# Normalising and transposing the second half of the rows in the head, and storing raw queries from ScalarE's queue

## The chip, the cores and the metric

The kernel runs on one core of a Trainium2 chip. The metric is the device time of one launch in microseconds; a time given for a kernel is the median of its runs. The engines are named as in the profile: PE is TensorE (PEld its weight loads), DVE is VectorE, ACT is ScalarE, POOL is GpSimd, SP is SyncE, which here does nothing but issue DMAs.

## The reference

One layer of a transformer block on 1024 rows of 1024 features, all in float32, batch 1: three residual steps, each behind an RMS norm.

```python
x = x + _hybrid_mixer(_rms_norm(x, norm1_g[l]), w_in[l], ...)
x = x + _memory_xattn(_rms_norm(x, norm2_g[l]), mem, ...)
x = x + _sq_relu_mlp(_rms_norm(x, norm3_g[l]), w_ff_in[l], w_ff_out[l])
```

The hybrid mixer first projects the normed rows with `w_in` (1024 x 1760), and splits the result:

```python
proj = h @ w_in
c_q, c_kv, k_idx, w_idx, q_nsa, kv_nsa, g_nsa = jnp.split(proj, splits, axis=-1)
c_q = _rms_norm(c_q, dsa_cq_g)
c_kv = _rms_norm(c_kv, dsa_ckv_g)
q_d = _rope(_rms_norm((c_q @ w_dsa_uq).reshape(B, L, DSA_HEADS, D), dsa_qn_g), pos)
k_d, v_d = jnp.split(c_kv @ w_dsa_ukv, 2, axis=-1)
q_i = _rope((c_q @ w_idx_q).reshape(B, L, IDX_HEADS, IDX_DIM), pos)
q_n = _rope(_rms_norm(q_nsa.reshape(B, L, NSA_HEADS, D), nsa_qn_g), pos)
```

Then every block of 128 rows attends in four ways: over 256 keys that an indexer selects by top-k (`q_i` scores, `q_d` attends), over keys compressed from blocks of 32, over 16 selected blocks of 64, and over a window of 512. All are causal: a block of rows needs keys of its own and of earlier rows alone. The result goes through `w_out`. Memory cross-attention (4 heads, 256 memory rows) and an MLP with squared ReLU (width 4096) follow.

## The kernel before

**Tiles and parts.** The 1024 rows are 8 tiles of 128 rows, and these are two parts of four: `PARTS = ((0, 4), (4, 4))`. Part 0 is projected first, in a stretch called the head here, with pools of its own (`p1` in SBUF, `ps1` in PSUM). Then these pools close, the main pools open, and two streams are interleaved: attention of tile after tile (`attend`), and a `fill` of everything else: projection of part 1 (in a pool `p2`), the memory stage, what lies between, and a first part of the MLP. Attention of tiles 4 to 7 is held until part 1 is projected. After that comes the tail, mostly MLP.

**Order of the work.** Each stream is a Python generator that yields the price of what it has just issued, and the streams are merged by these prices: `alternate` takes from the stream that is behind, `chain` runs one after the other, `drain` runs one out, and `together` (from L110) lets the fill run up to a pace beside attention, or alone while attention is held. A planner at build time then orders the instructions of each engine by its own estimate of times. On the chip each engine, and each engine's DMA queue, works through its own list in order: a DMA that waits for its data holds every DMA behind it on the same queue.

**project(pool, part, pe, st)**, from L370, does one part:

- The gain of the norm is loaded, broadcast to all partitions (L337, 512 KB). Then for each of four tiles, x is loaded (L375, 512 KB) and `norm_T` runs: ACT squares and sums (L285), DVE scales the sum (L229), POOL raises it to the power -1/2 (L231), DVE multiplies by that and by the gain (L287), PE transposes in eight blocks of 128 x 128 (L274), and ACT and DVE copy the two halves from PSUM (in part 0 split into a high and a low f32r part, L235 and L236; in part 1 kept whole as f32, L278 and L280).
- Eleven constants are loaded (L384 to L394).
- The columns of `w_in` are multiplied in this order: keys and values to be compressed; `c_q`, then `c_kv` with the indexer's key and the gates; keys and values of the selected blocks and of the window, with `compress` beside (part 0) or behind (part 1); `w_dsa_ukv`; NSA queries with `k_prep` (the keys' norms and rotation); then `w_dsa_uq` and `w_idx_q`. Matrix multiplications are at L218. Part 0 uses three multiplications of split operands; part 1 multiplies whole f32 weights (loaded at L265 into buffers named wlo and whi; one step shows as two instructions).
- Raw queries go out through `stage_q` (L398 to L403): ACT copies each tile's 128 x 256 result from PSUM to a buffer `st` (L401), and after the fourth tile SP stores the buffer, 512 KB, to DRAM (L403). Six such stores belong to each part. `st` has two buffers in `p1` and one in `p2`.

Attention reads the stored queries back: `q_prep` (from L560) loads `qin` on SP (L564), normalises and rotates it on ACT, POOL and DVE (L574 to L584), and PE transposes it (L590).

The part of the kernel that calls all this, before the change:

```python
drain(project(p1, 0, pe, st))
...
yield from project(p2, part, pe, st)
```

Of the kernel before, what the change touches and what calls it, by code (L numbers as in the profile page):

```python
# [26 lines left out]
PARTS = ((0, 4), (4, 4))  # L27
# [56 lines left out]
def drain(gen):  # L84
    for _ in gen:
        pass
# [80 lines left out]
def build(nc, tc, I, C, out):  # L167
    v, s, g, te = nc.vector, nc.scalar, nc.gpsimd, nc.tensor
    ctx = ExitStack()
    W = {n: I[n][0] for n in I}  # L170
# [4 lines left out]
    at_pool = tc.tile_pool(name="at", bufs=1, side="right", reuse_waits="tile")  # L175
    at = at_pool.__enter__()
    p1_pool, p1_psum = tc.tile_pool(name="p1", bufs=1, reuse_waits="tile"), tc.tile_pool(name="ps1", bufs=1, space=PSUM)
    p1 = p1_pool.__enter__()
    psum.update(pool=p1_psum.__enter__(), n=PSUMS["p1"])

# [4 lines left out]
    def ring(pool, tag, shape, dt=F32):  # L185
        n = RINGS[pool.name if isinstance(pool.name, str) else "dn"][tag]
        return pool.tile(shape, dt, tag=tag, name=tag, bufs=n)

    def row(ap):
        return ap[None, :]  # L190
# [91 lines left out]
    def norm_T(pool, x_t, gb, xs):  # L282
        ss = small(pool, "nss", 1)
        xn = ring(pool, "x4", [P, DM])
        s.activation(xn, x_t, AF.Square, accum_out=ss)  # L285
        r = rsqrt_of(pool, ss, DM, 1, "n")
        v.scalar_tensor_tensor(xn, x_t, r[:, 0:1], gb, op0=ALU.mult, op1=ALU.mult)  # L287
        to_T(pool, xn, xs, DM // P)
# [11 lines left out]
    def gemm(pool, xs, nk, nt, wsrc, chunks, consume):  # L300

        for ci, parts in enumerate(chunks):
            w = sum(n for _, n in parts)
            gr = []
            for k0 in range(0, nk, KG):
                kn = min(KG, nk - k0)
                srcs, o = [], 0
                for c0, n in parts:
                    srcs.append((lambda r, o=o, n=n: r[:, :, o:o + n],
                                 wsrc[k0 * P:(k0 + kn) * P, c0:c0 + n].rearrange("(k p) n -> p k n", p=P)))  # L310
                    o += n
                ws = load_w(pool, [P, kn, w], *srcs) if len(xs) == 2 else load_whole(pool, [P, kn, w], *srcs)
                gr += [[x[:, k, :] for x in ws] for k in range(kn)]
            for t in range(nt):
                pt = pst(TAGS[pool.name][0], [P, w])
                for k in range(nk):
                    if len(xs) == 1:
                        mm(pt, xs[0](t, k), gr[k][0], k == 0, k == nk - 1)
                        continue
                    wh, wl = gr[k]  # L320
                    xh, xl = xs[0](t, k), xs[1](t, k)
                    mm(pt, xh, wh, k == 0, False)
                    mm(pt, xh, wl, False, False)
                    mm(pt, xl, wh, False, k == nk - 1)
                consume(ci, t, pt)
                yield nk * (5 - len(xs)) * w / 2400.0

    def xT(pool, nt, whole=False):

        parts = [pool.tile([P, DM // P, nt * P], F32 if whole else F32R, tag="x" + n, name="x" + n)  # L330
                 for n in ("h" if whole else "hl")]
        return (parts, [lambda t, k, x=x: x[:, k, t * P:(t + 1) * P] for x in parts],
                lambda t: [x[:, :, t * P:(t + 1) * P] for x in parts])

    def gain(pool, src, tag="x4"):
        gb = ring(pool, tag, [P, DM])
        nc.sync.dma_start(gb, row(src).to_broadcast([P, DM]))  # L337
        return gb

    def gain2(pool, src):  # L340
        gs = [ring(pool, "h", [P, 512]) for _ in range(2)]
        for i, gb in enumerate(gs):
# [16 lines left out]
    qraw = [[[dr.tile([P, n, 256], F32, tag=f"q{k}{t}{c}", name=f"q{k}{t}{c}") for c in range(2)] for t, n in PARTS]  # L359
            for k in range(3)]  # L360
# [4 lines left out]
    xo_dr = [dr.tile([P, 512], F32, tag=f"xo{t}", name=f"xo{t}") for t in range(NT)]  # L365


    def project(pool, part, pe, st):
        t0, nt = PARTS[part]
        gb1 = gain(pool, W["norm1_g"])  # L370
        whole = part > 0
        _, xf, xt_of = xT(pool, nt, whole)
        for t in range(nt):
            x_t = ring(pool, "x4", [P, DM])
            nc.sync.dma_start(x_t, I["x"][0, (t0 + t) * P:(t0 + t + 1) * P, :])  # L375
            norm_T(pool, x_t, gb1, xt_of(t))
            yield 1.0
        cq = [ring(pool, "c8", [P, nt, 2, P], F32 if whole else F32R) for _ in xf]
        ckv = [ring(pool, "c4", [P, nt, P], F32 if whole else F32R) for _ in xf]
        kraw = [ring(pool, "kraw", [P, 6, 64]) for t in range(nt)]  # L380
# [15 lines left out]
        qst = []  # L396

        def stage_q(k, c, t, pt):  # L398
            if t == 0:
                qst[:] = [ring(pool, "st", [P, nt, 256])]  # L400
            s.activation(qst[0][:, t, :], pt, AF.Copy)  # L401
            if t == nt - 1:
                nc.sync.dma_start(qraw[k][part][c], qst[0])  # L403

        def consume(ci, t, pt):
            T = t0 + t
# [20 lines left out]
            if ci in (2, 3):  # L427
                stage_q(1, ci - 2, t, pt)
# [17 lines left out]
        def w_in(chunks, first):  # L446
            return gemm(pool, xf, DM // P, nt, W["w_in"], chunks,
                        lambda ci, t, pt: consume(ci + first, t, pt))
# [33 lines left out]
        yield from w_in([[(968, 256)]], 4)  # L482
        yield from w_in([[(0, 256)], [(256, 200), (1736, 24)]], 0)
        pair_ = (w_in([[(1224, 256)], [(1480, 256)]], 5), compress(pool, part, KT, pe, st, ctab))
        yield from (alternate if part == 0 else chain)(*pair_)
        yield from gemm(pool, [lambda t, k, c=c: c[:, t, :] for c in ckv], 1, nt,
                        W["w_dsa_ukv"], [[(0, 128)]], consume_kv)
        yield from alternate(w_in([[(456, 256)], [(712, 256)]], 2), k_prep())
        for k, name in ((0, "w_dsa_uq"), (2, "w_idx_q")):
            yield from gemm(pool, [lambda t, k, c=c: c[:, t, k, :] for c in cq], 2, nt,  # L490
                            W[name], [[(0, 256)], [(256, 256)]],
                            lambda ci, t, pt, k=k: stage_q(k, ci, t, pt))
# [568 lines left out]
    def pe_stack():  # L1061
        pe = p1.tile([P, 2, 32], F32R, tag="pe", name="pe")
        pe2 = ring(p1, "relu", [P, 2, 2, 64])
        for j in range(2):
            nc.sync.dma_start(pe2[0:32, :, j, :], W["nsa_cmp_pe"].rearrange("k l d -> l k d"))
        pp = pst("M", [P, 2, 32])
        for kv in range(2):
            te.transpose(pp[:, kv, :], pe2[0:32, kv, :, :].rearrange("p a d -> p (a d)"), ident[0:32, 0:32])
        s.activation(pe, pp, AF.Copy)
        v.tensor_tensor(pe[64:128], pp[64:128], pe[64:128], op=ALU.subtract)  # L1070
        return pe

    st = {
        "K": at.tile([P, 6, L], F32R, tag="K", name="K"),
        "V": [at.tile([P, NT, 2, 2, 64], F32R, tag=f"V{b}", name=f"V{b}") for b in range(2)],
        "Vd": at.tile([P, NT, 2, 64], F32R, tag="Vd", name="Vd"),
        "Kc": {},
        "Vc": {},
        "cT": [at.tile([64, 2, 64], F32, tag=f"cT{kv}", name=f"cT{kv}") for kv in range(2)],
        "cb": [at.tile([64, 1], F32, tag=f"cb{kv}", name=f"cb{kv}") for kv in range(2)],  # L1080
        "wi": at.tile([P, NT, 8], F32, tag="wi", name="wi"),
# [5 lines left out]
        v.memset(st["cT"][kv], 0.0)  # L1087
    pe = pe_stack()
    plan["w"] = PLAN_HEAD
    drain(project(p1, 0, pe, st))  # L1090
    plan["w"] = PLAN_MAIN
    p1_psum.__exit__(None, None, None)
    p1_pool.__exit__(None, None, None)
# [4 lines left out]
    projected = []  # L1098

    def fill():  # L1100
        for part in range(1, len(PARTS)):
            with tc.tile_pool(name="p2", bufs=1, reuse_waits="tile") as p2:
                yield from project(p2, part, pe, st)
            projected.append(part)
        dn = dn_pool.__enter__()
        yield from memory(dn)
        yield 1, PACES[1]
        yield from between(dn, 0, 2, {}, False)
        yield 3, PACES[2]
        x2s = {}  # L1110
        yield from between(dn, 2, 2, x2s, True)
        yield 3, PACES[3]
        yield from mlp(dn, 0, 4, x2s)
        yield 5, PACES[4]
        yield from between(dn, 4, 2, {}, False)

    rest = fill()
    together(attend(aw, st), rest, projected)
    aw_pool.__exit__(None, None, None)
# [32 lines left out]
```

## Time and profile before

| | |
|---|---|
| median of 3 runs | 1833.72 us (1833.55 to 1837.51) |
| profiled execution | 1835.75 us, its span 1833.9 us |
| PE busy | 1726.9 us, 94% of the span |
| ACT, DVE, POOL busy | 59%, 51%, 49% |
| mean granted TensorE clock | 0.970 |
| DMA | 187.50 MB, mean 102 GB/s |

PE busy is the time in which at least one matmul is under way. A row of an engine's timeline gives the start, the duration, the engine, the line and operation, out<-in by the names in the program, shapes and a count, and in brackets the idle time before it with what ended it. A row of groups gives the busy time and the mean duration in ns, then the idle time just before. A row of DMA issues gives the count, the KB of each and the median time from issue to landing. SPq is the DMA queue of SP.

### The profile page before, as it was taken

What the parts mean: (1) busy time and instruction counts of PE and PEld (TensorE: products, weight loads), DVE (VectorE), ACT (ScalarE), POOL (GpSimd) and SP (SyncE); (2) the same over time, 40 slices, a digit from 0 to 9 for tenths busy, and PEclk for the clock granted to TensorE, in tenths of its full rate; (3) what the DMA queues carried; (4) which work ended last, traced back from release to release, by engine and by line L of the source; (5) the groups of instructions that cost most, each with busy time, mean ns of one, the idle gap of its engine ahead of it and who ended that gap; (6) DMA issues with size and microseconds to landing.
All of it is one profiled execution on the core that took longest, in us unless ns stands there. A gap on an engine that the chain in (4) does not pass through costs nothing. (4 is left out here: it accounts for less than half of the span.)

```text
span 1833.9 us, 28049 instructions
## 1 busy us (share of the span) xinstructions
PE 1726.9 (94%) x9262; PEld 1474.2 (80%) x9262; DVE 936.1 (51%) x2353; ACT 1074.6 (59%) x2687; POOL 895.0 (49%) x1034
## 2 busy tenths in 40 slices
PE   5996999889989998999999999999999799999999
PEld 5995988777878787778887788888988578787787
DVE  4553766575684678466664656646523422222222
ACT  4444658889588669955797457994412323333332
POOL 2364657446262244677676576662111144454443
PEclk9997998999999999999999999999989799999999
DMA  8224512256335320222112112125394222222232
GB/s 203 70 87 160 103 34 79 78 193 180 122 112 162 120 81 24 73 81 71 64 63 91 54 65 75 60 79 185 99 288 131 71 69 92 92 93 93 94 99 98
DMA packets 180081, 187.50 MB, mean 102 GB/s; under 512 B 34656, under 2 KB 149088, under 8 KB 179936
## 3 DMA queue, kind: packets, MB, share of 16 engines
q1 hardware_dynamic: 172000, 175.23, 30.8%
q0 software_dynamic: 7936, 10.49, 2.2%
q8 instruction: 73, 1.20, 0.3%
q14 instruction: 72, 0.59, 0.1%
HBM read 164.69 MB, written 20.97 MB: 101 GB/s over the span
## 5 line engine op out<-in xcount | busy, mean ns | idle before, releaser
L249 POOL TENSOR_TENSOR wlo<-wraw,whi 128x512 fp32r<-128x512 f32 (+1 forms) x230 | 308.5, 1347 | 278.7 <-ACT whi L244 247.6
L244 ACT ACTIVATE whi<-wraw 128x512 fp32r<-128x512 f32 (+2 forms) x289 | 181.1, 628 | 247.4 <-PE psS L218 147.1
L218 PE MATMUL psD<-whi,xh 128*128 128x256 f32 (+1 forms) x704 | 193.8, 359 | 3.6 <-ACT whi L244 2.9
L218 PE MATMUL psD<-wlo,xh 128*128 128x256 f32 (+1 forms) x704 | 194.8, 357 | 0.8 <-DMA wlo<-in_w_in_dram 0.8
L236 DVE TENSOR_TENSOR pl<-psPT,ph 128x512 fp32r<-128x512 f32 (+1 forms) x232 | 142.2, 621 | 78.2 <-ACT ph L235 75.4
L218 PE MATMUL psD<-whi,h 128*128 128x512 f32 x512 | 174.3, 404 | 1.8 <-POOL h L1037 1.0
L688 ACT ACTIVATE S<-S,mn 128x128 f32<-128x128 f32 (+7 forms) x192 | 142.7, 744 | 41.5 <-DVE mn L686 40.3
L218 PE MATMUL psS<-whi,h 128*128 128x512 f32 x512 | 162.1, 392 | 5.1 <-DVE b L899 5.1
L693 POOL TENSOR_SCALAR S<-S,sums,gi 128x640 f32<-128x640 f32 (+7 forms) x128 | 107.7, 850 | 106.7 <-DVE sums L691 99.0
L235 ACT ACTIVATE ph<-psPT 128x512 fp32r<-128x512 f32 (+1 forms) x232 | 122.8, 540 | 60.9 <-PE psPT L703 54.5
L249 DVE TENSOR_TENSOR wlo<-wraw,whi 128x512 fp32r<-128x512 f32 (+1 forms) x59 | 64.3, 1090 | 166.9 <-ACT whi L244 166.8
L218 PEld LDWEIGHTS psD<-whi,xh 128*128 128x128 f32 x704 | 134.0, 198 | 14.3 <-ACT whi L244 3.3
L218 PEld LDWEIGHTS psD<-wlo,xh 128*128 128x128 f32 x704 | 134.8, 197 | 12.5 <-DMA wlo<-in_w_in_dram 1.2
L703 PE MATMUL psPT<-c_ident,S 128*128 128x128 f32 x816 | 132.3, 279 | 8.3 <-DVE ql L236 4.2
L899 DVE TENSOR_TENSOR b<-psS,b 128x512 f32<-128x512 f32 (+1 forms) x80 | 50.0, 635 | 152.6 <-PE psS L218 152.6
L218 PEld LDWEIGHTS psS<-whi,h 128*128 128x128 f32 x512 | 96.1, 188 | 29.3 <-DVE b L899 9.3
L218 PE MATMUL psS<-K,qh 128*128 128x384 f32 (+3 forms) x288 | 113.5, 397 | 5.6 <-DVE mn L686 2.8
L218 PEld LDWEIGHTS psD<-whi,h 128*128 128x128 f32 x512 | 95.6, 190 | 23.7 <-DVE b L899 1.5
L703 PEld LDWEIGHTS psPT<-c_ident,S 128*128 128x128 f32 x816 | 98.1, 143 | 18.9 <-POOL S L693 5.6
L218 PE MATMUL psD<-wlo,h 128*128 128x512 f32 x256 | 102.5, 404 | 1.3 <-POOL wlo L249 1.3
L218 PE MATMUL psD<-xh,wlo 128*128 128x512 f32 x256 | 101.5, 398 | 0.0
L899 DVE TENSOR_TENSOR b<-psD,b 128x512 f32<-128x512 f32 (+1 forms) x112 | 63.2, 572 | 74.5 <-PE psD L218 73.0
(299 smaller groups left out, 4647.4 us busy)
## 6 DMA issues: line engine op xcount, KB each, us to landing
wraw<-in_w_ff_in_dram SPq DMA_DIRECT2D x128, 256.0 KB, 2.7
wraw<-in_w_ff_out_dram SPq DMA_DIRECT2D x128, 256.0 KB, 2.6
whi<-in_w_out_dram SPq DMA_DIRECT2D x32, 256.0 KB, 5.0
wlo<-in_w_out_dram SPq DMA_DIRECT2D x32, 256.0 KB, 4.6
wraw<-in_w_in_dram SPq DMA_DIRECT2D x24, 256.0 KB, 3.1
q<-st SPq DMA_DIRECT2D x12, 512.0 KB, 2.6
qin<-q SPq DMA_DIRECT2D x44, 128.0 KB, 2.3
x<-in_x_dram SPq DMA_DIRECT2D x8, 512.0 KB, 5.2
```

The lines of the kernel that those rows point to most:

```text
L218: te.matmul(o, a, b, start=start, stop=stop)
L235: s.activation(hi, src, AF.Copy)
L236: v.tensor_tensor(lo, src, hi, op=ALU.subtract)
L244: s.activation(hi, raw, AF.Copy)
L249: (v if l == "v" else g).tensor_tensor(lo, raw, hi, op=ALU.subtract)
L688: s.activation(S, S, AF.Exp, bias=low, scale=-1.0, accum_out=sums[:, hh:hh + 1])
L693: g.tensor_scalar(Ss[hh], Ss[hh], sums[:, hh:hh + 1], 1.0 if gate is None else gate[:, hh:hh + 1], op0=ALU.mult, op1=ALU.mult)
L703: te.transpose(p2[:, j, hh, :], S[:, (c + j) * P:(c + j + 1) * P], ident)
L899: v.tensor_tensor(dst, pt, dst, op=ALU.add)
```

## The change

Three things are done:

1. The norm and the transposes of part 1 are taken out of `project` into a generator `normed`. The head norms tiles 0 to 3 first, and then runs `normed` for tiles 4 to 7 as a third stream beside the projection of the keys and values of the selected blocks and of the window, and beside `compress`. The transposed rows of tiles 4 to 7 (`xf1`, 16 KB per partition) lie in a new pool `pre`, which stays open until part 1 is projected. The fill's `project` gets `xf1` and begins with its constants.
2. The gain of the norm is loaded once rather than twice.
3. The stores of raw queries, all twelve, are issued from ACT's DMA queue rather than SP's.

```diff
+    pre_pool = tc.tile_pool(name="pre", bufs=1, reuse_waits="tile")
+    pre = pre_pool.__enter__()
     p1 = p1_pool.__enter__()
...
-    def project(pool, part, pe, st):
+    def normed(pool, part, gb1, xt_of):
         t0, nt = PARTS[part]
-        gb1 = gain(pool, W["norm1_g"])
-        whole = part > 0
-        _, xf, xt_of = xT(pool, nt, whole)
         for t in range(nt):
             x_t = ring(pool, "x4", [P, DM])
             nc.sync.dma_start(x_t, I["x"][0, (t0 + t) * P:(t0 + t + 1) * P, :])
             norm_T(pool, x_t, gb1, xt_of(t))
             yield 1.0
+
+    def project(pool, part, pe, st, xf, beside_it):
+        t0, nt = PARTS[part]
+        whole = part > 0
...
             if t == nt - 1:
-                nc.sync.dma_start(qraw[k][part][c], qst[0])
+                s.dma_start(qraw[k][part][c], qst[0])
...
-        yield from (alternate if part == 0 else chain)(*pair_)
+        yield from (alternate if part == 0 else chain)(*pair_, *beside_it)
...
-    drain(project(p1, 0, pe, st))
+    gb1 = gain(p1, W["norm1_g"])
+    _, xf0, xt_of0 = xT(p1, PARTS[0][1])
+    _, xf1, xt_of1 = xT(pre, PARTS[1][1], True)
+    drain(normed(p1, 0, gb1, xt_of0))
+    drain(project(p1, 0, pe, st, xf0, [normed(p1, 1, gb1, xt_of1)]))
...
     def fill():
-        for part in range(1, len(PARTS)):
-            with tc.tile_pool(name="p2", bufs=1, reuse_waits="tile") as p2:
-                yield from project(p2, part, pe, st)
-            projected.append(part)
+        with tc.tile_pool(name="p2", bufs=1, reuse_waits="tile") as p2:
+            yield from project(p2, 1, pe, st, xf1, [])
+        projected.append(1)
+        pre_pool.__exit__(None, None, None)
```

## The prediction

> **What bounds the kernel now.** I read the busy table first, then windows of 20 us, then the instructions around the one deep dip.
>
> ```profile
> span 1833.9 us, 28049 instructions
> PE 1726.9 (94%) x9262; PEld 1474.2 (80%) x9262; DVE 936.1 (51%) x2353; ACT 1074.6 (59%) x2687; POOL 895.0 (49%) x1034
> 140.00:160.00 20.00, 7.24 (x50) 6.27 (x49) 3.27 (x8) 4.79 (x12) 5.19 (x6) 0.73 0.58 192
> 160.00:180.00 20.00, 18.30 (x84) 15.56 (x85) 10.21 (x40) 11.27 (x35) 13.72 (x25) 0.76 0.51 174
> 340.00:360.00 20.00, 17.35 (x87) 13.22 (x85) 7.86 (x17) 19.40 (x65) 7.73 (x12) 1.00 0.16 63
> 360.00:380.00 20.00, 16.90 (x76) 12.67 (x76) 14.41 (x51) 14.64 (x44) 3.80 (x6) 0.91 0.38 136
> 380.00:400.00 20.00, 16.16 (x84) 13.70 (x83) 14.33 (x42) 17.62 (x53) 11.07 (x17) 0.83 0.77 256
> ```
>
> TensorE bounds it: 94% busy, 107 us idle in all. A window row gives its length, then PE, PEld, DVE, ACT and POOL busy, the granted clock, the DMA share and GB/s. The dip at 140:160 is the seam, where the head (projection of tiles 0 to 3) has ended and the fill (projection of tiles 4 to 7) has to begin. The three rows from 340 are the stretch where attention waits for that second projection: ACT, at 19.40 of 20, is the busiest engine there, and PE loses 2.65 + 3.10 + 3.84 us. The seam in detail (start, duration, engine, line, out<-in, count, then idle before and its releaser):
>
> ```profile
> 144.76 0.28 PE L218 MATMUL psD<-whi,c 128*128 128x256 f32 x1
> 156.43 1.09 PE L274 MATMUL psM<-c_ident,x 128*128 128x128 f32 x4 [11.39 <-DVE x L287]
> 158.20 1.12 PE L274 MATMUL psM<-c_ident,x 128*128 128x128 f32 x4 [0.69 <-ACT xh L278]
> 160.10 2.07 PE L218 MATMUL psD<-wlo,xh 128*128 128x256 f32 x4 [0.78 <-DMA wlo<-in_w_in_dram]
> 163.68 1.06 PE L590 MATMUL psPT<-c_ident,qd 128*128 128x128 f32 x4
> 144.88 1.21 ACT L401 ACTIVATE st<-psD 128x256 f32<-128x256 f32 x4 [2.30 <-DMA q<-st]
> 132.30 14.14 SPq L403 DMA_DIRECT2D q<-st  x5
> 146.54 0.37 SPq L337 DMA_DIRECT2D x<-in_norm_g_dram  x1
> 146.97 0.78 SPq L375 DMA_DIRECT2D x<-in_x_dram  x1
> 149.25 0.43 SPq L386 DMA_DIRECT2D pc<-in_c_ccos_dram  x1
> 150.19 3.54 SPq L394 DMA_DIRECT2D pc<-in_nsa_kn_g_dram  x4
> 155.20 0.43 SPq L265 DMA_DIRECT2D wlo<-in_w_in_dram  x1
> ```
>
> The head's last matmul ends at 145.04. SP stands from 132.30 in five raw-query stores, each held by its last ACT copy; only behind them go the gain, x, eleven constants and the first weight (155.20). x then needs landing, square, power, multiply, transpose. PE idles 11.39 + 0.69 + 0.78 = 12.9 us.
>
> **The change, part by part.** The sums are made against the profiled execution: span 1833.9 us, 1835.75 with what lies around it, 2.0 above the median of 1833.72. I apply the difference to the median.
>
> Moved norms. Their prices in the head, where tiles 0 to 3 do the same:
>
> ```profile
> L285 ACT ACTIVATE x<-x 128x1024 f32<-128x1024 f32 x4 | 4.2, 1058 | 6.6 <-DMA x<-in_x_dram 6.6
> L287 DVE SCALAR_TENSOR_TENSOR x<-x,nr,x 128x1024 f32<-128x1024 f32 x4 | 6.2, 1545 | 1.8 <-POOL nr L231 1.8
> 40.00:60.00 20.00, 20.00 (x179) 20.00 (x178) 12.52 (x33) 10.88 (x35) 8.59 (x10) 1.00 0.71 142
> 60.00:80.00 20.00, 20.00 (x178) 20.00 (x178) 10.21 (x33) 9.28 (x31) 7.18 (x8) 1.00 0.09 28
> ```
>
> Per tile some 1.6 us of DVE and 1.8 of ACT with one copy each, in windows where these have 7 to 11 us of 20 free; the four x loads (SP, 0.8 us at most each) find a DMA share of 0.09 at 60:80. Those cost nothing, covered by PE's own matmuls; without that cover a tile's chain would show as at the seam. The 32 transposes take PE itself, which is full: eight took 1.09 + 1.12 us at half clock, hence about 1.07 at full, 4.3 us in all. The head ends 4.3 us later, near 149.3, and the fill does 4.3 us less: 0 in sum. A head bubble is bounded by 0 and 1.7 us (6.6 over four, what each load kept ACT waiting in that row); I take 0, as the later loads find quieter queues. The second gain load (0.37 us of SP, 512 KB) goes; it was hidden among the seam's other issues.
>
> The seam itself. What is late next: constants and weights are still issued after the head, since only norms and x loads were moved. The stores leave SP's queue, so SP no longer waits for ACT in order. But in the program as built, one of the last constants still waits for the landing of the head's last raw-query store (the DMAs share a fixed set of completion semaphores, and this one's previous user is that store); already before, four L394 issues took 3.54 us where single ones take 0.43. Counting from the head's last matmul: last copy 1.05 (146.09 minus 145.04), store issue 0.35, landing 2.6, four constants 1.7, weight issue 0.4 and landing 3.2: 9.3 us. The stores' and weights' rows, and the chain that follows:
>
> ```profile
> q<-st SPq DMA_DIRECT2D x12, 512.0 KB, 2.6
> wlo<-in_w_in_dram SPq DMA_DIRECT2D x12, 256.0 KB, 3.2
> qin<-q SPq DMA_DIRECT2D x44, 128.0 KB, 2.3
> 154.05 0.40 ACT L574 ACTIVATE qta<-qin 128x256 f32<-128x256 f32 x1
> 159.30 0.96 POOL L584 TENSOR_TENSOR qd<-qta,qtb 128x256 f32<-128x256 f32 x1
> ```
>
> So 9.3 us of idle in place of 12.9: -3.6. Attention's first query is issued behind four weights (1.9 us), lands 2.3 later and needs 6.2 us of preparation (154.05 to 160.26): 16.4 us after the head's end, while PE has 16 matmul pairs ready at half clock, 9.3 + 7 = 16.3. That bubble is between 0 and 2.5; I take 1. Against it, tiles 5 to 7's norms no longer interrupt 163 to 182, where the two windows of 174:182 show clocks of 0.80 and 0.78:
>
> ```profile
> 162.00:166.00 4.00, 4.00 (x13) 3.26 (x12) 1.95 (x4) 2.16 (x4) 0.65 (x2) 0.50 1.06 339
> 174.00:178.00 4.00, 2.76 (x13) 2.08 (x14) 2.15 (x16) 2.52 (x11) 3.92 (x7) 0.80 0.33 131
> 178.00:182.00 4.00, 4.00 (x22) 3.80 (x22) 2.97 (x8) 2.62 (x8) 3.14 (x8) 0.78 0.10 33
> ```
>
> Between 0 and 3 (1.2 us of idle and 1.7 of lost clock); I take 0.9, as attention's own waits lie there too. The half clock after the gap (0.50 until 166) stays, since the gap stays long. Seam: -3.6 + 1 - 0.9 = -3.5, between -6.6 and 0.
>
> Stores on ACT. Six fall into the head, six between 325 and 374, five of them in the second and third row:
>
> ```profile
> L403 SPq DMA_DIRECT2D q<-st x12: 319/320/439, 118.6 to 373.2; - x12
> 347.16 6.92 SPq L403 DMA_DIRECT2D q<-st  x2
> 359.93 13.63 SPq L403 DMA_DIRECT2D q<-st  x3
> 373.66 1.22 SPq L343 DMA_DIRECT2D h<-in_mem_norm_g_dram  x2
> PEld psD L218 <- ACT st L401: 5.4, 5, 2.5
> 386.93 0.41 PE L703 MATMUL psPT<-c_ident,S 128*128 128x128 f32 x2 [3.06 <-DVE ql L236]
> ```
>
> An issue costs SP 0.32 to 0.44 us. In the head ACT has half of its time free: 0. Later it hasn't (19.40 at 340:360): 6 x 0.35 = 2.1 us. Queued behind each store are the next top-k steps and the next copy, which must wait for the landing in the one staging buffer (its ring is 1 there, before as after), with 5 to 9 ACT instructions in between. The extra is between 0 (hidden by PE's own queue) and 6 x (0.35 + 2.5, the longest wait of PE's weight load on such a copy) = 17; I take 2.1, nearest to the issue rows, because the landing wait existed before.
>
> "The Trainium skill", page "DMA: Bandwidth & Descriptors", section "Issuing engines are not separate DMA queues", says that all issuing engines feed the same 16 DMA engines and that spreading saves only the sequencer's issue time. By that rule the queue change is worth 12 x 0.32 = 3.8 us of an SP that isn't the bound, so nothing; the trace's 14.14 us for five issues shows in-order waiting on top of issue time, which the rule leaves out.
>
> Freed SP at 347 to 373. It stood 20.5 us in stores; behind them were the memory stage's loads (373.66), and PE then idles 6.9 us in 360:400. They can go out earlier, giving PE work in those gaps. Also the second projection, 32 transposes shorter, is interleaved further ahead of attention, so less of it runs alone against ACT. Between 0 and 6.9; I take 2.3, a third, since most waits there (the 3.06 on ql) are attention's own and only lack fill beside them.
>
> Sum: -3.5 + 2.1 - 2.3 = -3.7: 1832.05 for a profiled execution like this one, 1830.0 at the median.
>
> **The rivals.**
> ACT stores stall (slower). Place: 325 to 375. For: ACT 19.40 of 20 and PE's waits on L401 already there. Against: 5 to 9 ACT instructions stand between a store and the next copy, and the landing wait existed before. It decides once a store costs over 1.2 us (6 x 1.2 = 7.2 against 3.5 from the seam, and no gain from SP). At 2 us each: +12 - 3.5 = +8.5, 1842.
> The cover is spent early (slower). Place: after 400. The fill, ahead by the moved steps, is used up sooner beside attention, and later gaps of attention lie open:
>
> ```profile
> 400.00:1000.00 600.00, 575.02 (x3140) 488.29 (x3139) 365.01 (x963) 462.98 (x1172) 325.00 (x385) 0.99 0.32 96
> 1000.00:1480.00 480.00, 456.60 (x2387) 388.41 (x2386) 247.31 (x599) 256.56 (x558) 200.70 (x212) 0.95 0.34 108
> 1480.00:1833.90 353.90, 345.03 (x1492) 279.08 (x1490) 89.48 (x104) 110.53 (x182) 168.09 (x145) 1.00 0.29 94
> ```
>
> PE idles 25.0 and 23.4 us in the first two. Opened by 4.3 us, and as much again at half clock after them, this is +8.6 - 3.7 = +4.9: 1838.6. It decides from 3.7 us. For: the build order moves all later work. Against: much MLP work is left at 1480.
> The full seam goes (faster). If weights land before the head ends, the 12.9 us of idle go, with 1.5 us of slow clock and nothing lost on ACT: -14.4 + 1.2 for the query's late start, -13.2, 1820.5. Against: the store whose landing a constant awaits.
> Nothing moves. The constants keep SP as long as x did, seam 0, ACT's 2.1 against SP's 2.3: 1833.7. The rule quoted above points here for the queue's part.
>
> **How the numbers follow.** Small gain 0.42, own range 1825 to 1834 (0.24 below 1830.05, 0.18 above); stalls on ACT 0.22; cover spent 0.15; full seam 0.14; nothing 0.07. About 0.2% (3.7 us) is what a measurement can tell from no change. Faster 0.24 + 0.14 = 0.38; same 0.18 + 0.07 = 0.25; slower 0.22 + 0.15 = 0.37. The range runs from the full seam, 1820, to a little above the ACT rival, 1844; stalls near the bound of 17 and gains beyond the full seam are left out.
>
> **What would show it.** The seam: head's last matmul near 149.3, the next PE work about 9 us later and released by a weight's DMA, not by L287; the clock 0.50 there as before. No L285 between 146 and 182, four more near 30 to 80. Stores: ACTq rows at L406, a top-k step late by one issue each; a wait "ACT st <- DMA q<-st" of over 1 us in 340:375 would speak for the first rival. Memory loads before 370 show the freed SP. It is wrong if PE's idle past 400 differs by over 4 us from 25.0 and 23.4, or the gap is under 4 or over 12.

## The result

The changed kernel takes 1888.03 us (median of four runs, 1885.15 to 1893.02) against 1835.28 us for the kernel before in the same comparison: a ratio of 1.029, 95% interval 1.0263 to 1.0316. The change costs 53 us. The prediction was 1830.0 us with a range of 1820 to 1844, so it was wrong in size and in sign.

The first lines of the profile after, and its windows of 20 us that answer to those shown of before (columns as there):

```profile
span 1891.2 us, 28024 instructions
PE 1749.3 (92%) x9262; PEld 1493.0 (79%) x9262; DVE 942.1 (50%) x2353; ACT 1076.3 (57%) x2687; POOL 886.7 (47%) x1034
140.00:160.00 20.00, 12.94 (x108) 12.56 (x106) 5.70 (x12) 7.28 (x19) 4.97 (x6) 0.97 0.36 140
160.00:180.00 20.00, 14.65 (x66) 12.75 (x66) 2.81 (x6) 3.36 (x7) 4.37 (x7) 0.78 1.00 204
340.00:360.00 20.00, 18.98 (x110) 15.65 (x110) 12.95 (x38) 18.85 (x64) 9.49 (x16) 1.00 0.25 85
360.00:380.00 20.00, 7.06 (x31) 5.28 (x30) 5.26 (x17) 16.97 (x53) 4.84 (x9) 0.76 0.60 205
380.00:400.00 20.00, 20.00 (x99) 17.58 (x97) 13.05 (x41) 9.65 (x26) 5.50 (x9) 0.90 0.82 249
```

PE executes as many instructions as before (9262), is busy 22.4 us longer (1749.3 against 1726.9, the same instructions at a mean granted clock of 0.955 rather than 0.970) and idle 34.9 us longer (141.9 against 107.0). Together these are the 57.3 us between the two spans.

The seam, in rows of the timelines of PE, SP and ACT after the change, and then what SP's queue waited for in 138 to 160 (us in total, times, longest):

```profile
154.02 0.28 PE L220 MATMUL psD<-whi,c 128*128 128x256 f32 x1
165.35 3.70 PE L220 MATMUL psD<-wlo,xh 128*128 128x256 f32 x8 [11.05 <-DMA wlo<-in_w_in_dram]
174.07 0.60 PE L593 MATMUL psPT<-c_ident,qd 128*128 128x128 f32 x4
...
149.04 10.02 SPq L397 DMA_DIRECT2D pc<-in_nsa_kn_g_dram  x4
160.58 0.38 SPq L267 DMA_DIRECT2D wlo<-in_w_in_dram  x1
162.54 0.47 SPq L567 DMA_DIRECT2D qin<-q  x1
...
154.75 0.33 ACTq L406 DMA_DIRECT2D q<-st  x1
...
SPq L397 <- DMA q<-st: 13.6, 4, 4.9
```

The head's last matmul ends at 154.30, 9.3 us later than before, and PE then idles 11.05 us where it idled 12.9. The gap is released by the weight, no longer by the norm. SP is held by the landings of the raw-query stores, which are on ACT's queue: four issues of L397 take 10.02 us and end about 4 us after the last store's issue. The first query of attention, loaded at 147.84 before, is loaded at 162.54. For PE the seam alone is near neutral: in 0 to 300 us it executes 1770 instructions, and 1783 before. So most of the loss lies further on.

Where it begins is read from attention. Every tile from 2 on needs a top-k, which picks the keys that it attends to: index scores (PE, ACT, DVE), then 32 steps on ACT, each of which needs the one before it. The two rows below are the first top-k step of tile 3, before and after, and then the stores of attention's output, all 64, with the time of the first and the last, before and after:

```profile
388.13 0.29 ACT L645 ACTIVATE tks<-tko,tkg 128x1 f32<-128x1 f32 x1
L717 SPq DMA_DIRECT2D o<-oc x64: 574/586/1124, 186.8 to 1330.6; - x64
```

```profile
425.91 0.28 ACT L648 ACTIVATE tks<-tko,tkg 128x1 f32<-128x1 f32 x1
L720 SPq DMA_DIRECT2D o<-oc x64: 574/580/994, 202.5 to 1384.3; - x64
```

Attention starts 15.7 us later, tile 3's top-k 37.8 us later, and the last output is stored 53.7 us later. What follows it hardly changes: the span ends 503.3 us after the last store before, 506.9 us after the change, and between 500 and 507 us in every kernel of the next section. The end of attention carries the difference.

Between the end of tile 2's top-k and the start of tile 3's lie 25 us before and 50 after (363 to 388, 376 to 426). PE's groups in 363 to 403, before and then after:

```profile
L218 PE MATMUL psS<-K,qh 128*128 128x384 f32 x13 | 5.5, 421 | 0.3 <-ACT ir L612 0.2
L218 PE MATMUL psD<-whi,xh 128*128 128x256 f32 x16 | 5.0, 444 | 0.0
L218 PE MATMUL psD<-wlo,xh 128*128 128x256 f32 x12 | 4.0, 464 | 0.0
```

```profile
L220 PE MATMUL psD<-whi,xh 128*128 128x256 f32 x36 | 10.2, 410 | 0.0
L220 PE MATMUL psD<-wlo,xh 128*128 128x256 f32 x34 | 9.9, 410 | 0.0
L276 PE MATMUL psM<-c_ident,relu 128*128 128x128 f32 x19 | 4.3, 345 | 11.4 <-DVE relu L299 10.7 <-ACT xh L280 0.7
L220 PE MATMUL psS<-K,qh 128*128 128x384 f32 x5 | 2.1, 414 | 0.0
```

The psD<-..,xh of this stretch are the memory stage's keys and values, which attention does not need. They took 9.0 us of PE before, all from 389 on, when tile 3's index scores were done, and 20.1 after; attention's psS<-K,qh fell from 13 to 5. The six last index steps of tile 3 on ACT, the first and the last of them, before and after:

```profile
368.03 0.60 ACT L612 ACTIVATE ir<-psS 128x512 f32<-128x512 f32 x1 [1.48 <-DVE isc L616]
380.13 0.59 ACT L612 ACTIVATE ir<-psS 128x512 f32<-128x512 f32 x1
```

```profile
383.75 0.60 ACT L615 ACTIVATE ir<-psS 128x512 f32<-128x512 f32 x1 [2.55 <-DVE isc L619]
413.96 0.57 ACT L615 ACTIVATE ir<-psS 128x512 f32<-128x512 f32 x1
```

They are 12.1 us apart before and 30.2 after. PE takes its list in order. In the lists as built, no memory matmul stands ahead of the eighth and last index matmul of tile 3 before the change, and 48 do after it (96 rows of the trace, two to a matmul, between 380 and 411). The memory stage comes early against attention: its loads (in_mem_norm_g first) are issued at 365.15 rather than 373.66, while tile 2's top-k runs until 376 rather than 363. That the loads come earlier because the second projection is shorter by the moved norms is argued, not shown.

The two windows that follow, from 400 to 1000, are those of the changed kernel and of the same kernel with the tie described below. PE idles 46.1 us in the first, and 25.0 before the change, so 21 us of its 34.9 us of added idle time lie here, behind the delay at tile 3:

```profile
400.00:1000.00 600.00, 553.89 (x2971) 470.80 (x2970) 364.31 (x966) 440.47 (x1121) 304.81 (x374) 0.96 0.29 88
400.00:1000.00 600.00, 572.51 (x3134) 487.63 (x3133) 367.46 (x976) 464.06 (x1181) 320.98 (x385) 0.99 0.32 98
```

### The profile page after: what moved, and what is told of

Read it like the earlier page. It is cut to its first block, busy times and chain, and to the rows that moved or that the text cites. A ratio compares the mean times of both kernels' runs of the same rounds, so it can differ in the third digit from the quotient of the medians.

```text
span 1891.2 us, 28024 instructions
## 1 busy us (share of the span) xinstructions
PE 1749.3 (92%) x9262; PEld 1493.0 (79%) x9262; DVE 942.1 (50%) x2353; ACT 1076.3 (57%) x2687; POOL 886.7 (47%) x1034
## 5 line engine op out<-in xcount | busy, mean ns | idle before, releaser
L220 PE MATMUL psS<-xh,whi 128*128 128x512 f32 x256 | 101.3, 397 | 0.0
```

The source lines that it names most:

```text
L220: te.matmul(o, a, b, start=start, stop=stop)
```

## The experiments

Three theories stood at the start. A: attention starts late at the seam. B: the six stores on ACT beside the top-k steps. C: the four price units that the norms had in the merge of fill and attention are gone from the fill, so the fill runs ahead. Theory D, the memory matmuls between tile 3's index scores, came from the traces of the first four runs; E stands for any new order costing something. Ratios are to the kernel before, with 95% intervals.

**Norms moved alone.**

```diff
-                s.dma_start(qraw[k][part][c], qst[0])
+                nc.sync.dma_start(qraw[k][part][c], qst[0])
```

> The changed kernel with its twelve raw-query stores back on SP's queue (the norms stay in the head). Theory A (attention is the stream that decides; it starts 15 us late at the seam, and that lateness grows to 53 us at its end): SP again stands in order behind the stores, the first query is loaded no earlier than 160 us, and the time stays at 1870 to 1895 us. Theory B (the six stores on ACT beside the top-k steps cost it): the 10.7 us gap near 366 goes and the time falls below 1850 us. Theory C (the fill, four price units shorter, runs ahead of attention): as with A, 1870 to 1895 us.

Measured: 1890.61 us, 1.0289 (1.026 to 1.0317). With the stores back on SP the whole loss remains, so B is not its cause. The first top-k step of tile 3 comes at 417, the last output at 1382.6. The memory loads are issued at 362.28, earlier than before the change, though SP is not freed of its stores.

**Stores moved alone**, the same edit in the kernel before, the other way.

> The kernel before with only the twelve stores moved to ACT's queue (norms in the fill as before). Theory A: SP reaches the first query no later than before (147.84 us), so 1825 to 1845 us. Theory B: the stores' cost shows in full, 1860 us or more. Theory C: price units are as before, so 1825 to 1845 us, as with A.

Measured: 1848.41 us, 1.0065 (1.0042 to 1.0089). No theory had this: a cost, but a fifth of what B needs. PE's waits on the staging copies in 320 to 380 are as before (5.5 and 3.6 us in place of 5.4 and 3.8), so the stores don't stall it there. Tile 3's top-k starts 3 us later, tile 5's 9, and the last output is 10 us later. No memory matmul stands between tile 3's index matmuls in this trace, so theory D does not explain this cost either.

**The four price units put back**, and **twenty**.

```diff
     def fill():
+        yield 4.0
         with tc.tile_pool(name="p2", bufs=1, reuse_waits="tile") as p2:
```

> The changed kernel with the four price units that the norms had in the fill put back as one empty step of 4.0 at the fill's start, so that attention is let ahead as far as before. Theory C: most of the loss goes, 1835 to 1855 us. Theory A: the first query still waits behind constants and landings on SP; at most a few us of the 15 come back, 1870 to 1890 us. Theory B: no change, 1880 to 1895 us.

> The same with an empty step of 20.0, so that attention is issued well ahead of the fill from its start. Theory A: the first query and attention's first steps go ahead of constants and weights, attention starts by 155 to 165 us, and 15 us or more come back: 1840 to 1870 us. Theory C: as good or better, 1830 to 1860 us. Theory B: no change, 1880 to 1895 us.

Measured: 1867.58 us, 1.017 (1.0141 to 1.0198), and 1866.79 us, 1.0153 (1.0122 to 1.0183). Four units bring 20 us back, twenty no more. With four, attention's first query goes ahead of the weights and the first output is stored at 185.5, earlier than before the change (186.8); yet the last comes at 1359.2. So A falls as the main cause (the time with twenty lies in its range, but the start of attention was back with four), and C is a part: some 30 us remain. About half of them appear between tiles 2 and 3: with four units tile 2's top-k ends at 360, earlier than before the change (363), and tile 3's begins at 403, 15 us later; the rest gathers in later tiles.

**The tie.** The loads of the memory rows wait until the index scores of tile 3 are complete; nothing else is changed in the kernel's text.

```diff
         v.tensor_tensor(acc[:, t * P:Wd], acc[:, t * P:Wd], causal[:, 384:512], op=ALU.subtract)
+        if t == 3:
+            st["gate"] = small(aw, "gate", 1, bufs=1)
+            v.tensor_copy(st["gate"], acc[:, t * P:t * P + 1])
...
             x_t = ring(pool, "b4", [P, DM])
+            v.tensor_copy(x_t[:, 0:1], st["gate"])
             nc.sync.dma_start(x_t, I["mem"][0, t * P:(t + 1) * P, :])
```

> The changed kernel, with one tie added: the loads of the memory rows wait for a one-column copy that DVE makes when the index scores of tile 3 are complete, so that no matmul of the memory stage can stand between the index matmuls of tile 3 in PE's list (as built, 0 of them between the first and the eighth, as in the kernel before; 48 in the changed one). Theory D (memory's matmuls, early because the second projection ends early, hold up tile 3's index scores, and with them attention's serial top-k chain): the first top-k step of tile 3 comes 15 to 25 us earlier than 426 us, and the time falls by as much, to 1863 to 1875 us. Theory C (the four price units alone): no change, 1880 to 1895 us. Theory E (any new order costs something, without one place): no change, or a change without relation to the first top-k step.

Measured: 1849.76 us, 1.0075 (1.0052 to 1.0098): 38 us of the 53 are gone, more than expected. Two windows, the index steps' first and last of the six, and the stores of attention's output, with the tie:

```profile
360.00:380.00 20.00, 4.69 (x17) 3.04 (x16) 6.71 (x20) 13.49 (x42) 2.81 (x5) 0.73 0.70 220
380.00:400.00 20.00, 15.96 (x80) 12.64 (x79) 16.87 (x57) 14.24 (x42) 9.82 (x15) 0.84 0.14 45
377.72 0.60 ACT L615 ACTIVATE ir<-psS 128x512 f32<-128x512 f32 x1 [4.43 <-DVE isc L619]
391.94 0.60 ACT L615 ACTIVATE ir<-psS 128x512 f32<-128x512 f32 x1
L723 SPq DMA_DIRECT2D o<-oc x64: 574/581/615, 199.8 to 1343.9; - x64
```

PE idles more in this stretch than in the changed kernel, 19.4 us of these 40 against 12.9, and yet the kernel is 38 us faster; over the whole span PE's idle time is lower, 119.3 us against 141.9. The index steps take 14.2 us rather than 30.2, tile 3's top-k starts at 399 rather than 426, and the last output comes 40 us earlier. So D holds in this pair: the memory stage's early place costs the 38 us. (Other pairs, below, are less simple.) In the traces without the second tie (below), the last four index matmuls of tile 3 begin within 8 to 11 us where no memory matmul stands between them, and within 21 to 24 where some do. One thing the tie does not separate: as built, it also gives the lists of tiles 4 to 7 the same counts of fill instructions between index matmuls as before the change (49, 74, 122 and 153 in the second half of each; 34, 44, 127 and 142 without the tie). So 27 us stand at tile 3, and the other 13 may come from either. The second may be the prediction's rival that cover is spent early: with the tie PE idles 27.5 us in 400 to 1000 (second window above) in place of 46.1.

**The tie and the four units.**

> The same tie, together with the empty step of 4.0 at the fill's start. Theory D with C: the first top-k step of tile 3 by 392 us (403 without the tie), and 1840 to 1855 us. C alone: 1860 to 1870 us as without the tie. E: within 1855 to 1880 us without relation to that step.

Measured: 1841.26 us, 1.0033 (1.0021 to 1.0046); tile 3's top-k starts at 388, as before the change.

**The units alone, in the kernel before**, and **the same with the tie**.

```diff
             norm_T(pool, x_t, gb1, xt_of(t))
-            yield 1.0
+            yield 0.0 if whole else 1.0
```

> The kernel before, with the four norms of tiles 4 to 7 priced at 0 rather than 1.0 each in the merge of fill and attention; nothing is moved and no store changes its queue. As built, 16 memory matmuls stand between tile 3's index matmuls. Theory C: 1850 to 1860 us, as putting the 4.0 back gained 20 us. Theory D: the index scores are stretched by 16 of 48 matmuls, 1840 to 1850 us. If the moved norms themselves (head, seam) make the loss: 1832 to 1840 us.

> The kernel before, with the norms of tiles 4 to 7 priced at 0 and with the tie of the memory loads. Without the tie it took 1852.2 us (16 more than before) with 32 fill instructions between the middle and the last index matmul of tile 3; as built there are 0 now, and in the lists of tiles 4 to 7 the counts are those of the kernel before. If the units cost only through those memory matmuls (theory D): 1834 to 1842 us. If they cost by letting the fill ahead of tile 2's scores too (1186 against 1148 fill instructions): 1842 to 1850 us.

Measured: 1852.2 us, 1.0089 (1.0067 to 1.0112), and 1843.64 us, 1.0041 (1.0021 to 1.0061). A kernel in which nothing is moved, and only a price in the merge is changed, loses 16 us; the tie takes about half of it back. So units and memory matmuls are partly one cause. The other half may be the fill ahead of tile 2's scores: 1186 fill instructions stand before their last matmul, against 1148.

**Step and stores on SP; step, tie and stores on SP; tie and stores on SP.**

> The changed kernel with the empty step of 4.0 and with the stores back on SP's queue, so that only the moved norms differ from the kernel before in work and queues. If the stores on ACT cost the 11 us here that they cost alone: 1853 to 1860 us. If they cost nothing once the norms are moved (as with 1890.6 against 1888.0): 1862 to 1870 us. Theory D: 21 memory matmuls stand between tile 3's index matmuls, as against 31 with the stores on ACT, so 2 to 5 us less, 1862 to 1866 us.

> The changed kernel with the 4.0 step and the tie, all stores on SP. Against 1841.3 us with the stores on ACT and 1844.6 us with stores on SP but without the tie. Theory D: no memory matmul between tile 3's index matmuls, so its first top-k step comes by 390 us rather than 402, and the time is 1832 to 1842 us. If the stores' queue matters by itself: over 5 us away from 1841.3.

> The changed kernel with the tie and all stores on SP, without the 4.0 step. With the stores on ACT it took 1849.8 us. If ACT stores cost what they cost with step and tie (5.7 us): 1842 to 1847 us. If nothing, as without step and tie: 1848 to 1853 us.

Measured: 1844.57, 1835.57 and 1845.52 us. The first is 8 us below the lowest range of its expectation. The eight kernels with the norms in the head, as ratios to the kernel before:

| | stores on ACT | stores on SP |
|---|---|---|
| as changed | 1.0290 | 1.0289 |
| 4.0 step | 1.0170 | 1.0054 |
| tie | 1.0075 | 1.0044 |
| step and tie | 1.0033 | 1.0004 (0.9987 to 1.0021) |

With step, tie and the stores on SP, the moved norms cost nothing and gain nothing. The stores on ACT cost 0 to 12 parts in a thousand, depending on the rest: 21 us with the step alone, 5 us where the tie keeps the memory matmuls out. With the step alone the list has 31 rather than 21 memory matmuls between tile 3's index matmuls, for which theory D gave 2 to 5 us. The traces do not put the 21 us there: tile 3's top-k starts 1.5 us later with the stores on ACT (403.4 against 401.9), tile 7's 14.7 (1147.7 against 1133.0), and the last output comes 20.7 later. What makes the stores' cost grow from tile to tile is not shown.

Nor is a delay at tile 3 always carried to the end. Of the two kernels with step and stores on SP, the one without the tie starts tile 3's top-k 17 us later (401.9 against 384.9), but its last output comes only 5.6 us later (1338.5 against 1332.9). With step and tie a cost of the stores of 3 parts in a thousand is left; its intervals (1.0021 to 1.0046 against 0.9987 to 1.0021) only touch.

**The tie in the kernel before.**

> The kernel before with the tie alone. Its list has no memory matmul between the index matmuls of tile 3 from the fifth to the eighth in any case, so theory D says no change: 1830 to 1842 us. A gain of over 0.5% would mean that the tie helps for another reason, and that the 38 us it gave in the changed kernel aren't those of the index scores.

Measured: 1840.12 us, 1.0027 (1.0014 to 1.004). The tie by itself costs a little. Its 38 us in the changed kernel are no general gain.

**The constants in the head**, with step and tie: all eleven loaded once for both parts. With all stores on ACT, and with those of part 1 on SP.

```diff
+    ct = tables(pre)
+    drain(project(p1, 0, pe, st, xf0, [normed(p1, 1, gb1, xt_of1)], ct))
...
+            yield from project(p2, 1, pe, st, xf1, [], ct)
...
+                (s if part == 0 else nc.sync).dma_start(qraw[k][part][c], qst[0])
```

> The changed kernel with the 4.0 step and the tie, and with the eleven constants loaded once, in the head, for both parts (they are the same), so that SP has only weights and queries to issue at the seam. If the constants behind the last store's landing keep the seam open, as predicted: the first weight and the first query are issued 4 us or more earlier relative to the head's last matmul, PE's idle there shrinks from 9 us to 5 or less, and the time is 3 to 8 us below the 1841.3 us without it: 1833 to 1838 us. If the seam matters no longer once attention is fed in time: 1839 to 1843 us.

> The same with the six stores of part 1 issued from SP again, those of part 0 from ACT. If the stores on ACT beside the top-k steps cost time (rival of the prediction, and 12 us when the stores alone were moved): 4 to 12 us less than the kernel with all stores on ACT. If they cost only through the order of the later work: within 3 us of it.

Measured: 1842.47 us, 1.0035 (1.0022 to 1.0048), and 1838.96 us, 1.0026 (1.0008 to 1.0044). The gap after the head's last matmul falls to 5.1 and 4.8 us, as the step in the prediction implied, and the time stays about where it was. The seam's gain doesn't reach the end. In the kernel with step, tie and stores on SP it can be followed; the two windows before and in that kernel:

```profile
0.00:300.00 300.00, 259.85 (x1783) 242.98 (x1784) 166.63 (x497) 156.44 (x497) 147.57 (x219) 0.94 0.41 109
300.00:400.00 100.00, 90.41 (x467) 75.40 (x466) 67.66 (x191) 88.07 (x281) 53.59 (x74) 0.94 0.35 118
```

```profile
0.00:300.00 300.00, 265.54 (x1841) 247.59 (x1842) 173.58 (x511) 164.39 (x524) 151.09 (x225) 0.97 0.42 109
300.00:400.00 100.00, 82.94 (x409) 68.39 (x408) 64.73 (x182) 79.92 (x251) 47.26 (x70) 0.85 0.37 118
```

PE gains 5.7 us until 300, then loses 7.5 until 400. It has run through the second projection there, and stands 7.4 us in one wait for ACT's copy of tile 3's index scores (ir, L615), which comes behind tile 2's top-k (its last step is at 357.9, the copy at 362.64).

**A second tie**, that should start attention's top-k earlier: in the second projection, the loads from the fifth column block on wait for tile 2's index scores. The `yield` of a pair also stops the whole fill in the merge until attention has reached tile 2, so the edit does more than tie loads. It was made in the kernel with step, tie, constants in the head and part 1's stores on SP, and in the kernel with step, tie and all stores on SP.

```diff
+        if whole:
+            yield 1, PACES[0]
+            tie.append(None)
         pair_ = (w_in([[(1224, 256)], [(1480, 256)]], 5), compress(pool, part, KT, pe, st, ctab))
...
+        if len(tie) == 2:
+            v.tensor_copy(raw[:, 0, 0:1], tie[0])
+            tie.clear()
...
+        if t == 2:
+            tie.append(small(aw, "gate2", 1, bufs=1))
+            v.tensor_copy(tie[0], acc[:, t * P:t * P + 1])
```

> The kernel with the 4.0 step, the tie of the memory loads, the constants in the head and part 1's stores on SP, and a second tie: in the second projection, the loads from the fifth column block of w_in on wait until the index scores of tile 2 are complete. As built 1090 fill instructions stand before the last index matmul of tile 2 (1221 without it, 1148 in the kernel before). If the start of attention's serial top-k chain decides (theory D): first top-k step of tile 2 by 265 to 275 us in place of 286, attention's last store below 1328 us, and 1818 to 1832 us. If PE's total decides: PE idles more before 280 us while it waits for attention, and the time is 1838 to 1850 us.

> The same second tie in the kernel with the 4.0 step, the tie of the memory loads and all stores on SP, the constants as in the changed kernel. 1090 fill instructions before the last index matmul of tile 2, as against 1187. Theory D: 1820 to 1834 us, a few us behind the kernel with the constants in the head because of the longer gap at the seam. PE's total: 1836 to 1850 us.

Measured: 1860.2 us, 1.0137 (1.0123 to 1.015), and 1852.74 us, 1.0097 (1.0078 to 1.0116). Tile 2's top-k does start at 258 and 257, and tile 3's at 382 and 376, all earlier than before the change; and both kernels are slower than without it, outside every range expected. This goes against an early top-k as the one thing that decides. PE's windows with the second tie and all stores on SP, and then without it:

```profile
200.00:300.00 100.00, 91.14 (x518) 79.80 (x517) 67.52 (x255) 78.98 (x280) 62.38 (x107) 0.95 0.15 44
400.00:1000.00 600.00, 565.81 (x3032) 477.91 (x3031) 356.56 (x933) 448.57 (x1133) 303.60 (x364) 0.97 0.32 99
```

```profile
200.00:300.00 100.00, 97.69 (x599) 87.97 (x598) 67.70 (x246) 69.30 (x248) 67.50 (x113) 1.00 0.24 66
400.00:1000.00 600.00, 572.36 (x3111) 485.41 (x3110) 363.42 (x956) 461.51 (x1168) 315.48 (x378) 0.98 0.32 95
```

PE loses 6.6 us while attention runs alone before 300, gains 7.0 back until 400 (89.96 us busy against 82.94), and loses 6.6 after that. In attention, tile 7's top-k starts at the same time in both (1126.5 and 1126.7), and the last output comes 17 us later (1349.7 against 1332.9). So this loss arises behind the last top-k's start, and its cause was not found. No kernel here is faster than the kernel before.

## Why the prediction was wrong

- **Moved norms, 0 in sum.** The 32 transposes were put at 4.3 us; the head's end moved by 9.3. Up to it PE executes 32 instructions more (1030 against 998), is busy 7.2 us longer (129.07 against 121.92) and idle 2.1 us longer. Of the 7.2, about 3.2 are a lower granted clock in 80 to 120 (busy time of the windows of 20 us times what the clock lacks, against before; see the last section), so some 4 are the transposes. Their price was right; clock and waits were left out.
- **The seam, 9.3 us.** It measured 11.05, held by landings on SP as described. The first query was put at 16.4 us after the head's end and came at 19.8 (174.07), behind the weights. What the sum did not price is whom that delays: it counted the lateness as a bubble of PE (1 us), but attention's first output was 15.7 us late. The step of four units brings that start back, and 20 of the 53 us with it. (The 1.7 us of lost clock that the sum takes at 174 to 182 are 1.4 if the busy time of the two windows is used; this changes nothing.)
- **Stores on ACT, 2.1 us.** Alone they cost 12, with step and tie 5; the place given, waits of PE near 340 to 375, did not grow, and where the stores were moved alone no wait of ACT for a store's landing is recorded in 300 to 380. Mis-sized, and for a reason that the runs don't bear out; the right one is open.
- **"Freed SP", a gain of 2.3 us.** This is the step that failed. It said that memory loads going out earlier, and a fill interleaved further ahead of attention, give PE work in its gaps. Both happened, and the sign was the other way: that work stands in PE's list ahead of index matmuls on which a serial chain on ACT hangs. Holding the memory loads back gave 38 us. SP's freedom was not even needed for it: with the stores back on SP the loads come at 362.28, and the loss is whole. So it was the place of the fill in the order, its second half, that mattered. Of the 14 us or so that are left with the tie, the 4.0 units take back 7 to 8, which again hold the fill back, and the stores' return to SP's queue 5 to 6; then nothing of the loss remains.
- **The rivals.** "The cover is spent early" had the cause's name, the fill running ahead, and the sign given for it came: PE's idle time in 400 to 1000 is 46.1 us rather than 25.0. It put the price at 8.6 us, and it took the harm to be gaps left open later; that attention is delayed at once, by 27 us of tile 3's top-k that the tie takes back, it did not have. How much of the 13 us after tile 3 is spent cover stays open. The full seam and the stalls on ACT did not come.
- **The reading.** PE at 94% was taken as the bound, and each stage was summed by PE's idle time. The stretch from 340, read as attention waiting for the second projection, holds the top-k of tile 2 (279 to 363), then tile 3's index scores and, from 388, its top-k. That the last 503 us start where attention ends, and that attention hangs on such serial chains, is not to be seen in a sum of idle times.

## What to carry to other kernels

Where a filler stream shares an in-order engine with a stream that holds a serial chain, count what stands in that engine's list ahead of each step of the chain, before and after a change; making the filler shorter or earlier can be a loss, and a stretch in which the engine idles less can belong to the slower kernel. Look for a distance that stays constant from run to run (here from the last attention output to the end): what ends where it begins is what has to come earlier. The start of one link is not enough: the second tie brought two top-k starts forward and lost time. In a kernel whose order comes from a planner, change one price by itself as a control: here that alone moved the time by 16 us.

## What the runs showed of the hardware

The granted clock of PE fell to one half with no idle time at all. The windows of 2 us and two rows of PE's timeline of the changed kernel:

```profile
98.00:100.00 2.00, 2.00 (x21) 2.00 (x19) 0.00 (x0) 0.49 (x2) 0.00 (x0) 1.00 0.00 0
100.00:102.00 2.00, 2.00 (x14) 2.00 (x14) 1.04 (x2) 0.61 (x4) 0.73 (x1) 0.65 0.00 0
102.00:104.00 2.00, 2.00 (x10) 2.00 (x10) 0.76 (x1) 0.98 (x3) 0.75 (x2) 0.50 0.00 0
99.64 0.27 PE L220 MATMUL psC<-c,wlo 128*128 128x64 f32 x1
99.74 0.25 PE L220 MATMUL psM<-pe,whi 128*128 128x2 f32 x1
```

From 98 to 102 PE works almost only on matmuls of 64 and 2 columns, each with a weight load of its own, and is busy 2.00 of 2.00. From about 100.5 they become slower, and the wide matmuls that follow run at 0.50 until about 107. The kernel before shows it too, with 0.62 and 0.53 in 94 to 98 behind such matmuls. The Trainium skill, page "TensorE: Matmul & The Clock Gate", section "Part 1: The HAM clock gate", puts the half clock down to an idle window of some 3.4 us. The rows agree with that after the gap of 11.05 us at the seam, where the clock is 0.50 in 165 to 167. From 98 to 104 no idle time is recorded. A stretch of such narrow matmuls may count as idle; that was not tested by a run of its own.

One queue's issues can also be held by another queue's transfers: in this program SP's four L397 issues took 10.02 us, and the waits put down to them are for landings of the raw-query stores, which were on ACT's queue (13.6 us in four waits).
